# Feed-forward weights of a hybrid decoder trunk: one step of a weight strip at each of four places of a unit instead of three steps at each of two

## The chip, the cores and the metric

The kernel runs on one core of a Trainium2 chip. The metric is the device time of one execution in microseconds. Five engines work side by side, each through its own row of instructions in order: TensorE (PE, with PEld for its weight loads), VectorE (DVE), ScalarE (ACT), GpSimd (POOL) and SyncE (SP), which here mostly issues loads. An instruction that waits for another engine holds up all that stand behind it in its row.

## What is computed

One inference step of a decoder trunk of two layers, over 1048 positions in all (1024 prompt tokens, 16 meta tokens, and one token each of 8 running sequences). Each layer is a mixer (an SSD in layer 0, an RG-LRU in layer 1) and a feed-forward part, each inside norms and a residual. The change lies in the feed-forward part:

```python
D_MODEL = 1024
D_FF = 4 * D_MODEL

def sq_relu_mlp(x, w1, w2):
    h = jax.nn.relu(x @ w1)
    return (h * h) @ w2

# in trunk, behind the mixer of layer i
h = rms_norm(x, p["norm_ffn_pre"][i])
x = x + rms_norm(sq_relu_mlp(h, p["ffn_w1"][i], p["ffn_w2"][i]), p["norm_ffn_post"][i])
```

All inputs are f32. w1 is 1024 x 4096, w2 is 4096 x 1024.

## The kernel before

**Numbers as pairs.** A matrix goes to PE as two f16 matrices, a high part (the scaled value rounded to f16, written by ACT) and a low part (what the rounding left, written by DVE, which must read the high part first). A product is three matmuls: high by high, high by low, low by high. The scale of a weight strip is a power of two from the strip's largest entry.

**Tiles.** Positions stand in three pieces c of 350, 350 and 348 columns (`WC`). Weights come in strips of 256 output columns, 128 x 2048 in f32, 1 MB; a layer's feed-forward part has 32 of them. The hidden layer is worked through in four blocks b of 1024 columns: four strips of w1 make the block H, and four strips of w2 take it into `acc`. Except in the first block's w1 strips (`first_phase`, line 619, and a loop behind it) and the last block's w2 strips (`last_phase`, line 570), the work is done in units: `unit` (line 1357) is the product of one strip with one piece c by seven products of half-blocks in place of eight. Of the w1 strips (kind "H", b = 1 to 3) all four pairs of half-blocks go that way, 7 x 12 = 84 matmuls; of the w2 strips (kind "S", b = 0 to 2) two pairs do (`NSUM`), and the rest is added as ordinary products (`quadrant`), 90 matmuls. A matmul of a unit has 175 columns (174 for the last piece). The seven products go in the order 1, 6, 5, 7, 3, 4, 2 into four result buffers of PSUM, and there are eight such buffers, two units' worth. Between them ACT copies the first product into z (p1), and DVE adds the others up in z, in five or six rows: those are the rows `z<-z,mm` and `z<-mm,z`. Behind a unit of a w1 strip comes `square` (ReLU, square, the parts H, and for half the strips the sums HT that POOL makes in `t_sums`), behind one of a w2 strip an addition into `acc`.

**What a strip needs ahead of its units.** The generator `wlane` prepares strip after strip, in `wconv` (line 299), and every `yield` in it ends a step. In order: the load by SP into `ws` (two buffers, so a load waits until the strip two earlier has been split); the largest entry by DVE (`rm`, or `r4`, `r4s` and `rm` for kinds S and 2, where four parts have scales of their own); in `strip_scale` (line 267) a matmul that spreads that maximum over the partitions (`mm<-ident,rm`) and a chain of small DVE rows from `wgb` to the scales; for units, in `sums` (line 354), three quarters of the strip as high parts on ACT and low parts on DVE (`wp`), then four rows of POOL that turn the strip in `ws`, in place, into the sums that the unit's other products need; then in `split` (line 282) the whole strip as `wh`, the high part on ACT, which has to wait for POOL, and the low part in halves on DVE, which wait for ACT. For kind H that is one piece of 2048; for kinds S and 2 four pieces of 512. A finished strip goes into `ready`, and `wneed` takes it from there, running steps at once if there is none. `ahead` limits how many may stand ready.

**What sets the order.** All lanes are generators (the weight lane `wlane`, the sums of POOL, norms). `tick` (line 130) moves each of them by one step, and the weight lane by `wsteps` steps: 1 in general, 3 in the feed-forward part (set in line 1251, set back in `lru`). A unit calls `tick` once behind product 7, and `ffn` calls it once behind the unit: six steps of the weight lane a unit, 18 in the three units that a strip serves. A strip of kind H has 12 steps, of kind S 10, of kind 2 seven, of kind h (the first block's w1) three. `first_phase` and `last_phase` tick behind every group of products. The written order is not quite the order of the rows: every call goes through `Queue` (line 80 on), so all operations carry line 91, and a scheduler then settles the row of each engine.

## Time and profile before

| | |
|---|---|
| median of 3 runs | 2867.76 us (2867.46 to 2871.3) |
| the profiled execution, its own time | 2878.27 us |
| its span in the trace | 2876.5 us |
| mean granted clock of PE | 0.964 |
| unit stretch of layer 0 (first to last matmul of a unit) | 1094.75 to 1676.69, 581.94 us |
| unit stretch of layer 1 | 2183.70 to 2766.74, 583.04 us |
| PE busy over the span | 2601.7 us (90%) |
| DVE busy over the span | 2173.1 us (76%) |
| ACT, POOL busy over the span | 1322.5 us (46%), 662.3 us (23%) |
| loads of a strip, issue to landing | 64 of 1024 KB, 4.9 us |

Times in the trace run from the start of the span. A row of a view names the engine, the operation, the tile written and those read (without buffer numbers), the shape, and in brackets how long the engine stood idle just before and what ended that. Matmuls are pipelined, so the sum of their single durations is more than the time that they take together; the pace of a row of matmuls is read from the starts.

### The profile page before, as it was taken

Reading aid. Unit: us, or ns where it says so; the run is one execution under the profiler, and the core shown is the slowest. Engines: PE = TensorE matmul, PEld = TensorE weight load, DVE = VectorE, ACT = ScalarE, POOL = GpSimd, SP = SyncE. Lnnn points to the kernel's source line nnn. Section 1 sums busy time; section 2 is a strip of 40 time slices with the busy share of each in tenths; the row PEclk is TensorE's granted clock in tenths of the full one; section 3 lists DMA queues with packets and bytes.
Section 4 is the critical chain, followed back from the end, with each engine's and each line's share of the span. In section 5 each row is a group of like instructions: output and inputs, shape, how many; then the busy total and the mean of one; then the engine's idle time right before and its main releaser. Section 6 shows DMA issues by size and latency. Waiting matters only on the chain.

```text
span 2876.5 us, 56770 instructions
## 1 busy us (share of the span) xinstructions
PE 2601.7 (90%) x23318; PEld 2073.5 (72%) x23318; DVE 2173.1 (76%) x5152; ACT 1322.5 (46%) x2148; POOL 662.3 (23%) x863
## 2 busy tenths in 40 slices
PE   5999999999999999879789899989999889889888
PEld 2666666666666669879789866655668888879866
DVE  6888977897764887678688689678787678677666
ACT  4544455455544364352342444577564353352342
POOL 3212211221111025431321200132024531221101
PEclk9999999999999999999989999999999999999999
DMA  3233233322345221111121033111221101011122
GB/s 141 78 105 111 86 103 111 110 86 102 110 175 218 98 76 40 37 45 45 40 85 69 31 109 123 60 39 49 101 92 43 45 31 60 31 45 45 45 72 93
DMA packets 52756, 229.14 MB, mean 80 GB/s; under 512 B 9056, under 2 KB 18416, under 8 KB 31632
## 3 DMA queue, kind: packets, MB, share of 16 engines
q1 hardware_dynamic: 46112, 190.81, 19.2%
q0 software_dynamic: 6384, 34.71, 3.0%
q8 instruction: 182, 2.98, 0.4%
q14 instruction: 78, 0.64, 0.1%
HBM read 186.28 MB, written 39.22 MB: 78 GB/s over the span
## 4 chain that ended last, share of the span: by engine, by line
DVE 33%; PE 30%; ACT 11%; POOL 10%; DMA 8%; issue 8%; SPq 0%; POOLq 0%; DVEq 0%; ACTq 0%
PE mm L91 25%; POOL ws L91 7%; DMA ws<-w 6%; DVE z L91 5%; DVE wh L91 4%; ACT wh L91 3%; PE yo L91 2%; DVE conv L91 2%; DVE wp L91 2%; ACT z L91 2%; DVE U L91 2%; DVE L L91 2%; DVE rm L91 2%; DVE xr L91 2%; POOL z L91 1%
## 5 line engine op out<-in xcount | busy, mean ns | idle before, releaser
L91 PEld LDWEIGHTS <-wh 128*128 128x128 f16 x17040 | 1499.8, 99 | 536.0 <-issue 105.2
L91 PE MATMUL mm<-U,wh 128*128 128x350 f16 (+3 forms) x7056 | 998.0, 298 | 18.7 <-ACT rr L91 11.7
L91 PE MATMUL mm<-H,wh 128*128 128x175 f16 (+5 forms) x5664 | 560.8, 254 | 11.5 <-DVE z L91 11.5
L91 PEld LDWEIGHTS <-wp 128*128 128x128 f16 x3888 | 322.3, 101 | 47.0 <-issue 23.3
L91 POOL TENSOR_TENSOR ws<-ws 128x256 f32<-128x256 f32 (+1 forms) x192 | 210.2, 1095 | 622.1 <-DVE wp L91 593.5
L91 DVE TENSOR_TENSOR z<-z,mm 128x175 f32<-128x175 f32 (+3 forms) x648 | 227.2, 371 | 49.1 <-ACT z L91 42.6
L91 PE MATMUL mm<-U,wp 128*128 128x175 f16 (+1 forms) x1728 | 154.1, 247 | 25.3 <-DVE z L91 25.2
L91 DVE SCALAR_TENSOR_TENSOR wh<-ws,s,wh 128x256 f16<-128x256 f32 x256 | 148.8, 628 | 23.5 <-ACT wh L91 23.4
L91 PE MATMUL mm<-TT,wh 128*128 128x175 f16 (+1 forms) x1728 | 160.8, 242 | 5.3 <-DVE wh L91 4.5
L91 DVE SCALAR_TENSOR_TENSOR wh<-ws,sq,wh 128x1024 f16<-128x1024 f32 x48 | 61.5, 1281 | 111.8 <-ACT wh L91 111.8
L91 DVE SCALAR_TENSOR_TENSOR wh<-ws,sw,wh 128x1024 f16<-128x1024 f32 x94 | 117.5, 1279 | 26.4 <-ACT wh L91 26.4
L91 ACT ACTIVATE z<-z,ti 128x700 f32<-128x700 f32 (+1 forms) x72 | 62.9, 874 | 149.8 <-DVE z L91 149.8
L91 DVE TENSOR_REDUCE rm<-ws 128x1 f32<-128x2048 f32 x40 | 91.3, 2284 | 51.7 <-DMA ws<-w 46.5
L91 PE MATMUL mm<-ident,rm 128*128 128x128 bf16 x99 | 22.4, 228 | 107.6 <-DVE z L91 71.4
L91 ACT ACTIVATE pre<-mm,undo 128x8 f32<-128x8 f32 (+1 forms) x104 | 46.6, 476 | 153.9 <-PE mm L91 153.9
L91 ACT ACTIVATE wh<-ws,s 128x512 f16<-128x512 f32 x128 | 85.4, 711 | 68.2 <-POOL ws L91 60.5
L91 DVE SCALAR_TENSOR_TENSOR conv<-pre,ssmall,conv 128x1072 f32<-128x1072 f32 x78 | 105.8, 1357 | 0.0
L91 PE MATMUL mm<-H,wp 128*128 128x175 f16 (+1 forms) x864 | 90.5, 241 | 16.3 <-DVE z L91 16.3
L91 ACT ACTIVATE wh<-ws,sw 128x2048 f16<-128x2048 f32 x47 | 93.7, 1998 | 16.9 <-DVE sw L91 14.7
L91 DVE TENSOR_SCALAR L<-L,ncs 128x128 f32<-128x128 f32 (+1 forms) x288 | 94.5, 372 | 8.9 <-DMA L<-csd 8.9
L91 DVE TENSOR_TENSOR ss<-ss,sqt 128x350 f32<-128x350 f32 (+3 forms) x154 | 76.4, 502 | 32.7 <-ACT sqt L91 31.7
L91 ACT ACTIVATE wh<-ws,sq 128x2048 f16<-128x2048 f32 x24 | 48.0, 2002 | 108.3 <-POOL ws L91 108.3
(284 smaller groups left out, 4234.1 us busy)
## 6 DMA issues: line engine op xcount, KB each, us to landing
ws<-w SPq DMA_DIRECT2D x64, 1024.0 KB, 4.9
ws<-w_ssd_in SPq DMA_DIRECT2D x24, 1024.0 KB, 7.0
L<-csd SPq DMA_DIRECT2D x64, 256.0 KB, 3.3
ws<-w_lru_in SPq DMA_DIRECT2D x12, 1024.0 KB, 4.8
xd<-xc POOLq DMA_DIRECT2D x6, 1400.0 KB, 5.0
xc<-xd SPq DMA_DIRECT2D x6, 1400.0 KB, 6.2
h<-ssd_h SPq DMA_DIRECT2D x8, 1024.0 KB, 4.9
bc<-bcd SPq DMA_DIRECT2D x8, 1024.0 KB, 4.9
```

The costliest lines, as they stand in the source:

```text
L91: r = f(*args, **kw)
```

## The change

`wsteps` is gone: `tick` moves every lane by one step. A new `wtick` moves the weight lane alone by one step, and `unit` calls it behind products 6 and 4, so that a unit has four places with a step each (behind products 6, 7 and 4, and behind the unit): 12 steps in three units. `first_phase` and `last_phase` of the feed-forward part have one step of the weight lane a tick in place of three.

A strip's steps are cut differently. The spreading matmul is split off `strip_scale` into `spread_max`, with a step's end between it and the small rows for the kinds of the feed-forward part. In `split` all high parts are one step and the low parts follow in one step (kinds H and h) or two (kinds S and 2), where a high part and its two low parts alternated. In `sums` the three pairs of kind H keep a step each; the two groups of kind S are one step together; the four rows of POOL are one step, with one empty step behind them. Steps now: H 9, S 9, kind 2 six, kind h four. The operations, their shapes and their number are the same.

```diff
@@ -123,17 +123,19 @@
         self.lanes = []
         self.last_tab = None
         self.mmi = 0
-        self.wsteps = 1
         self.yfs = {}
 
 
     def tick(self):
 
         for lane in list(self.lanes):
-            for _ in range(self.wsteps if lane is self.wl else 1):
-                if next(lane, self) is self:
-                    self.lanes.remove(lane)
-                    break
+            if next(lane, self) is self:
+                self.lanes.remove(lane)
+
+    def wtick(self):
+
+        if self.wl in self.lanes and next(self.wl, self) is self:
+            self.lanes.remove(self.wl)
 
     def drain(self):
         while any(l is not self.wl for l in self.lanes):
@@ -264,14 +266,19 @@
         self.nc.sync.dma_start(st, src)
         return st
 
-    def strip_scale(self, gmax):
-
+    def spread_max(self, gmax):
+
+
+        ps = self.mm()[:, :P]
+        self.nc.tensor.matmul(ps, gmax.bitcast(BF16)[:, 1:2].to_broadcast([P, P]), self.ident.bitcast(BF16)[:, 1::2],
+                              start=True, stop=True)
+        return ps
+
+    def strip_scale(self, spread):
 
         nc, ty = self.nc, self.tiny
-        ps = self.mm()
-        nc.tensor.matmul(ps[:, :P], gmax.bitcast(BF16)[:, 1:2].to_broadcast([P, P]), self.ident.bitcast(BF16)[:, 1::2], start=True, stop=True)
         gb = ty.tile([P, 1], F32, tag="wgb", name="wgb")
-        nc.vector.tensor_reduce(gb, ps[:, :P], axis=AX.X, op=OP.max)
+        nc.vector.tensor_reduce(gb, spread, axis=AX.X, op=OP.max)
         s, p = self.pow2(gb, 1, ty, "w")
         inv = ty.tile([P, 1], F32, tag="winv", name="winv", bufs=8)
         nc.vector.tensor_scalar(inv, p, 2.0 ** -14, None, op0=OP.mult)
@@ -285,8 +292,11 @@
         for i in range(parts):
             sl = slice(i * step, (i + 1) * step)
             nc.scalar.activation(w[:, 0, sl], st[:, sl], AF.Copy, scale=s[:, i:i + 1])
-            yield
+        yield
+        for i in range(parts):
             h = step // 2
+            if i == 2:
+                yield
             for o in (i * step, i * step + h):
                 nc.vector.scalar_tensor_tensor(w[:, 1, o:o + h], st[:, o:o + h], s[:, i:i + 1], w[:, 0, o:o + h],
                                                op0=OP.mult, op1=OP.subtract)
@@ -327,7 +337,10 @@
             nc.vector.tensor_tensor(r4s, r4, rj, op=OP.mult)
             nc.vector.tensor_reduce(rm, r4s, axis=AX.X, op=OP.max)
         yield
-        s, inv, gb = self.strip_scale(rm)
+        spread = self.spread_max(rm)
+        if kind in "hH2S":
+            yield
+        s, inv, gb = self.strip_scale(spread)
         yield EARLY
         if kind != "a":
             w = new("wh")
@@ -371,13 +384,13 @@
                 nc.vector.scalar_tensor_tensor(lo, a, sk, hi, op0=OP.mult, op1=OP.subtract)
                 if parts == 1:
                     yield
+        if parts > 1:
             yield
         tt = nc.gpsimd.tensor_tensor
         for o, a, b, op in ((q(1, 1), q(1, 1), q(1, 0), OP.add), (q(1, 0), q(0, 0), q(1, 0), OP.subtract),
                             (q(0, 0), q(1, 1), q(0, 0), OP.subtract), (q(0, 1), q(0, 1), q(0, 0), OP.subtract)):
             tt(o, a, b, op=op)
-            if npair == 4:
-                yield
+        yield
         yield
 
     def product(self, ps, i, w, B, T, npair):
@@ -1248,7 +1261,6 @@
         HT = fp.tile([P, 3, NSUM, 3, 2, CW // 2], F16, name="HT")
         U = self.U
         sctx = ExitStack()
-        self.wsteps = 3
         for b in range(4):
             H = fp.tile([P, 3, KT, 2, CW], F16, tag="H", name="H")
             rs = {}
@@ -1381,12 +1393,14 @@
             if i == 6:
                 nc.scalar.activation(p1, pa[:, 0], AF.Copy)
                 nc.vector.tensor_tensor(u2, p1, pa[:, 1], op=OP.add)
+                self.wtick()
             if i == 7:
                 nc.vector.tensor_tensor(xy, pb, zv[:, 2:3].to_broadcast([P, 2, n]), op=OP.add)
                 nc.vector.tensor_tensor(u2, c12, pb[:, 1], op=OP.add)
                 self.tick()
             if i == 4:
                 nc.vector.tensor_tensor(xy, xy, pc, op=OP.add)
+                self.wtick()
         if npair < 4:
             self.chain(pd[:, 1], self.quadrant(w[0], B, npair, 1, 1))
         nc.vector.tensor_tensor(p1, p1, pd[:, 0], op=OP.add)
@@ -1396,7 +1410,6 @@
 
 
     def lru(self):
-        self.wsteps = 1
         nc, tc, ty = self.nc, self.tc, self.tiny
         a, v = self.a, self.v
         sctx = ExitStack()
```

Three places in DVE's row show what the scheduler made of it. Numbers in the names are those of buffers; they differ between the two programs for the same thing.

The first place is the third w1 strip of b = 1 in layer 0. `wp` and `wh` are the low parts of this strip, z_13553 the last unit of the strip in use, z_13673 and z_13797 (z_13799) the units behind it, mm the results of PE. DVE before, from two rows ahead of the last `wp` on:

```order
L91 TENSOR_TENSOR H_13295<-z_13553,H_13295 128x174
L91 TENSOR_TENSOR z_13673<-z_13673,mm_13670 128x175
L91 SCALAR_TENSOR_TENSOR wp_13729<-ws_13353,sq4_13730,wp_13729 128x512
L91 TENSOR_TENSOR HT_10777<-z_13553,HT_10777 128x3x174
L91 TENSOR_TENSOR z_13673<-z_13673,mm_13671 128x2x175
L91 TENSOR_TENSOR z_13673<-z_13673,mm_13672 128x175
L91 SCALAR_TENSOR_TENSOR wh_13728<-ws_13353,sq4_13730,wh_13728 128x1024
L91 TENSOR_TENSOR z_13797<-z_13797,mm_13793 128x175
L91 SCALAR_TENSOR_TENSOR wh_13728<-ws_13353,sq4_13730,wh_13728 128x1024
```

And DVE in the change, from the last `wp` on:

```order
L91 SCALAR_TENSOR_TENSOR wp_13703<-ws_13327,sq4_13704,wp_13703 128x512
L91 TENSOR_TENSOR z_13673<-z_13673,mm_13669 128x175
L91 TENSOR_TENSOR H_13295<-z_13553,H_13295 128x174
L91 TENSOR_TENSOR H_13295<-z_13553,H_13295 128x348
L91 TENSOR_TENSOR z_13673<-mm_13670,z_13673 128x2x175
L91 TENSOR_TENSOR z_13673<-z_13673,mm_13670 128x175
L91 TENSOR_TENSOR z_13673<-z_13673,mm_13671 128x2x175
L91 TENSOR_TENSOR H_13295<-z_13553,H_13295 128x174
L91 SCALAR_TENSOR_TENSOR wh_13702<-ws_13327,sq4_13704,wh_13702 128x1024
L91 TENSOR_TENSOR HT_10777<-z_13553,HT_10777 128x3x174
L91 TENSOR_TENSOR z_13673<-z_13673,mm_13672 128x175
L91 SCALAR_TENSOR_TENSOR wh_13702<-ws_13327,sq4_13704,wh_13702 128x1024
```

The last `wp` row, behind which POOL's four rows may run, has moved up past three rows of z_13673 and three H rows of z_13553, which now stand between it and the first `wh` row, and `HT` has moved from ahead of the first `wh` row to behind it. On POOL the four rows on `ws` stand ahead of the sums of z_13553 now, and behind them before.

The second place is the beginning of the unit stretch of layer 0: ws_11513 is the second w2 strip of b = 0, z_11715 (z_11696 in the change) the first unit of the first w2 strip, z_11851 the unit behind it, r the hidden values of the first block. DVE before:

```order
L91 SCALAR_TENSOR_TENSOR wp_11747<-ws_11513,s4_11752,wp_11747 128x128
L91 TENSOR_TENSOR H_10778<-r_11600,H_10778 128x2x350
L91 SCALAR_TENSOR_TENSOR wp_11747<-ws_11513,s4_11752,wp_11747 128x128 x5
L91 SCALAR_TENSOR_TENSOR wh_11746<-ws_11513,s4_11752,wh_11746 128x256 x8
L91 TENSOR_TENSOR z_11715<-z_11715,mm_11711 128x175
L91 TENSOR_TENSOR z_11715<-mm_11712,z_11715 128x2x175
L91 TENSOR_TENSOR H_10778<-r_11680,H_10778 128x2x348
L91 TENSOR_TENSOR z_11715<-z_11715,mm_11712 128x175
```

In the change:

```order
L91 SCALAR_TENSOR_TENSOR wp_11824<-ws_11513,s4_11829,wp_11824 128x128 x2
L91 TENSOR_TENSOR z_11696<-z_11696,mm_11695 128x175 x2
L91 SCALAR_TENSOR_TENSOR wp_11824<-ws_11513,s4_11829,wp_11824 128x128 x4
L91 TENSOR_TENSOR z_11851<-z_11851,mm_11847 128x175
L91 TENSOR_TENSOR z_11851<-mm_11848,z_11851 128x2x175
L91 SCALAR_TENSOR_TENSOR wh_11823<-ws_11513,s4_11829,wh_11823 128x256
L91 TENSOR_TENSOR z_11851<-z_11851,mm_11848 128x175
L91 SCALAR_TENSOR_TENSOR wh_11823<-ws_11513,s4_11829,wh_11823 128x256
L91 TENSOR_TENSOR U_9864<-f_11884,U_9864 128x175
L91 SCALAR_TENSOR_TENSOR wh_11823<-ws_11513,s4_11829,wh_11823 128x256 x3
L91 TENSOR_TENSOR z_11851<-z_11851,mm_11849 128x2x175
L91 SCALAR_TENSOR_TENSOR wh_11823<-ws_11513,s4_11829,wh_11823 128x256 x2
```

Before, all `wp` and `wh` rows of the second strip stand ahead of the first z row of the first unit; in the change they stand between the z rows of the first two units (the eighth `wh` row comes two rows later).

The third place lies in the w2 strips of b = 1 in layer 0: the last `r4` row reads a strip (ws_15146, in the change ws_15132) that is loaded into the buffer from which the strip two earlier (wh_14782, in the change wh_14768) has been split. z_14751 and z_14887 (z_14884) are units of the w2 strip in use. DVE before:

```order
L91 TENSOR_TENSOR z_14751<-z_14751,mm_14748 128x175
L91 SCALAR_TENSOR_TENSOR wh_14782<-ws_14450,s4_14788,wh_14782 128x256
L91 TENSOR_TENSOR z_14751<-z_14751,mm_14749 128x2x175
L91 SCALAR_TENSOR_TENSOR wh_14782<-ws_14450,s4_14788,wh_14782 128x256 x2
L91 TENSOR_TENSOR r4s_14995<-r4_14922,rj_13148 128x4
L91 TENSOR_REDUCE rm_14921<-r4s_14995 128x1
L91 TENSOR_TENSOR z_14751<-z_14751,mm_14750 128x175 x2
L91 SCALAR_TENSOR_TENSOR acc_10776<-z_14751,iq4_14456,acc_10776 128x700
L91 TENSOR_TENSOR z_14887<-z_14887,mm_14883 128x175
L91 TENSOR_TENSOR z_14887<-mm_14884,z_14887 128x2x175
L91 TENSOR_TENSOR z_14887<-z_14887,mm_14884 128x175
L91 TENSOR_REDUCE r4_15288<-ws_15146 128x2
```

In the change:

```order
L91 SCALAR_TENSOR_TENSOR wh_14768<-ws_14424,s4_14774,wh_14768 128x256 x5
L91 TENSOR_TENSOR z_14751<-z_14751,mm_14750 128x175 x2
L91 SCALAR_TENSOR_TENSOR wh_14768<-ws_14424,s4_14774,wh_14768 128x256
L91 SCALAR_TENSOR_TENSOR acc_10776<-z_14751,iq4_14430,acc_10776 128x700
L91 TENSOR_TENSOR z_14884<-z_14884,mm_14880 128x175
L91 SCALAR_TENSOR_TENSOR wh_14768<-ws_14424,s4_14774,wh_14768 128x256
L91 TENSOR_TENSOR z_14884<-mm_14881,z_14884 128x2x175
L91 TENSOR_TENSOR z_14884<-z_14884,mm_14881 128x175
L91 TENSOR_TENSOR z_14884<-z_14884,mm_14882 128x2x175
L91 TENSOR_REDUCE r4_15325<-ws_15132 128x2
```

The last `wh` row, which sets the load free, has moved from ahead of the last rows of z_14751 to behind the first row of the next unit, and the `r4` row that waits for the load has stayed within a row of where it was. SP's row holds the same loads in the same order in both.

## The prediction

> **What bounds the kernel now.** I began with the views that set the whole apart from its stages: the page's first line, then the busy time of each engine in the two stretches in which the units of the feed-forward part run (the two rows under it: stretch, its length, then busy time and instructions of PE, PEld, DVE, ACT and POOL, the granted clock, the DMA share, GB/s).
>
> ```profile
> span 2876.5 us, 56770 instructions
> 1094.75:1676.69 581.94, 506.37 (x6290) 499.69 (x6288) 436.50 (x1056) 223.11 (x393) 176.04 (x210) 0.94 0.15 52
> 2183.70:2766.74 583.04, 508.09 (x6290) 500.15 (x6288) 429.32 (x1051) 222.54 (x392) 175.90 (x210) 0.95 0.13 45
> ```
>
> The two stretches are 1165 of 2876.5 us, and only they, and the few us at their edges, are touched by the change in a way that can count: the rows of the SSD and LRU stages stand as before. The reader is to see that no engine is busy all the time, neither PE (506 of 582, and a busy PE includes slow matmuls) nor DVE (436). So the next view is the waits in the first stretch: engine, operation, what released it, us, times, longest.
>
> ```profile
> PE mm L91 <- DVE z L91: 59.3, 27, 8.1
> PE mm L91 <- DVE rm L91: 14.9, 4, 7.0
> DVE wh L91 <- ACT wh L91: 63.5, 22, 6.3
> DVE z L91 <- ACT z L91: 20.6, 18, 2.0
> DVE rm L91 <- DMA ws<-w: 16.6, 8, 3.0
> DVE r L91 <- DMA ws<-w: 5.8, 5, 2.0
> DVE z L91 <- PE mm L91: 2.1, 2, 1.3
> ```
>
> PE waits for DVE; DVE hardly ever waits for PE (2.1 us in 2 places). So **the row of DVE's work, its busy time plus its waits for ACT, POOL and DMA, is the stage**: 436.5 busy and some 145 idle, of which the 63.5 for ACT's high parts is the largest piece. Whatever shortens or lengthens that row counts, and PE follows. What the 63.5 is made of, the groups of DVE's instructions show (count, busy, mean ns, idle before).
>
> ```profile
> L91 DVE SCALAR_TENSOR_TENSOR wh<-ws,sq,wh 128x1024 f16<-128x1024 f32 x24 | 30.7, 1281 | 55.5 <-ACT wh L91 55.5
> L91 DVE SCALAR_TENSOR_TENSOR wh<-ws,s,wh 128x256 f16<-128x256 f32 x95 | 58.2, 654 | 8.1 <-ACT wh L91 8.1
> L91 DVE SCALAR_TENSOR_TENSOR wp<-ws,s,wp 128x128 f16<-128x128 f32 x60 | 18.6, 348 | 1.6 <-ACT wp L91 1.6
> L91 DVE TENSOR_TENSOR z<-z,mm 128x175 f32<-128x175 f32 x167 | 52.4, 331 | 14.1 <-ACT z L91 12.9
> L91 DVE TENSOR_TENSOR HT<-z,HT 128x522 f16<-128x522 f32 x4 | 5.8, 1445 | 0.9 <-ACT HT L91 0.8
> L91 DVE TENSOR_TENSOR HT<-z,HT 128x525 f16<-128x525 f32 x8 | 5.6, 705 | 5.0 <-ACT HT L91 5.0
> ```
>
> Twelve H strips (24 halves) cost 55.5 us of waiting, 4.6 each. One of them in order of time, the third of b=1 (start, us, engine, operation, count, idle before):
>
> ```profile
> 1226.40 0.81 DVE L91 SCALAR_TENSOR_TENSOR wp<-ws,sq,wp 128x512 f16<-128x512 f32 x1
> 1226.53 1.08 PE L91 MATMUL mm<-U,wh 128*128 128x174 f16 x12 [0.68 <-DVE z L91]
> 1227.34 5.63 POOL L91 TENSOR_TENSOR ws<-ws 128x512 f32<-128x512 f32 x4 [0.68 <-ACT HT L91]
> 1227.37 1.81 DVE L91 TENSOR_TENSOR HT<-z,HT 128x522 f16<-128x522 f32 x1 [0.16 <-ACT HT L91]
> 1227.45 1.07 PE L91 MATMUL mm<-TT,wh 128*128 128x174 f16 x12
> 1233.01 2.00 ACT L91 ACTIVATE wh<-ws,sq 128x2048 f16<-128x2048 f32 x1 [2.25 <-POOL ws L91]
> 1235.04 1.28 DVE L91 SCALAR_TENSOR_TENSOR wh<-ws,sq,wh 128x1024 f16<-128x1024 f32 x1 [5.20 <-ACT wh L91]
> 1236.63 0.26 PE L91 MATMUL mm<-ident,rm 128*128 128x128 bf16 x1 [8.11 <-DVE z L91]
> 1236.69 1.94 PE L91 MATMUL mm<-U,wh 128*128 128x174 f16 x12
> ```
>
> After DVE's last low part of the sums come 5.63 us of POOL and 2.00 of ACT: DVE needs 7.6 us of other work before its first wh row. What stands there I call the cover; here 2.3 us, and the wait is the rest. PE goes on until its result buffers are full and then stands for 8.11.
>
> **The change part by part.** No instruction is added or removed (the same maxima, copies, sums and matmuls), no new wait is written; all of it is order. So each term is DVE work moved into or out of a cover.
>
> *The chain of the H strips.* I laid the cover of all twelve strips side by side in the two orders, at the group means. A layer has 35.1 us before and 34.9 after: the third strip of b=1 gains 0.6 (seven z and H rows, 2.90, for HT and two z, 2.29), the last of b=3 gains 2.4, the fourth of b=1 loses 2.9 and that of b=2 1.7 (2.9 in the second layer). The largest wait of the stage is thus left where it is: +0.2 in layer 0 and +1.4 in layer 1, **+1.6**.
>
> *The reload of ws.* A strip may be loaded when the low parts of the strip two earlier are done, and its maximum is the next thing DVE wants:
>
> ```profile
> 1304.22 0.87 DVE L91 SCALAR_TENSOR_TENSOR wh<-ws,s,wh 128x256 f16<-128x256 f32 x2
> 1305.24 0.33 SPq L264 DMA_DIRECT2D ws<-w  x1
> 1305.27 0.58 DVE L91 TENSOR_TENSOR z<-z,mm 128x175 f32<-128x175 f32 x2
> 1305.88 0.95 DVE L91 SCALAR_TENSOR_TENSOR acc<-z,iq,acc 128x700 f32<-128x700 f32 x1
> 1306.75 0.33 DVE L91 TENSOR_TENSOR z<-z,mm 128x175 f32<-128x175 f32 x1
> ...
> 1310.12 1.22 DVE L91 TENSOR_REDUCE r<-ws 128x2 f32<-128x1024 f32 x1 [2.03 <-DMA ws<-w]
> ```
>
> From issue to the maximum are 4.9 us. Eight rows, 3.10 us at the group means, lie between, and the wait is 2.03. In the new order three z rows (1.36 us) lie there: 1.7 more of waiting. The same sum for the two strips ahead of it goes from 6.41 to 3.92 and from 4.29 to 2.91; against 4.9 us that adds 0.9 and 1.4. Together 4.0 at this place, and the same order stands at b=1 and b=2 of layer 1: **+12** for three places. The order of the loads on SP's queue doesn't change. Bounds: nothing, if the waits move into one another, and +17 if the lost cover counts in full (2.5+1.4+1.7, three times).
>
> *The second S strip of b=0.* Before, it is converted while the units have not yet begun to wait for DVE:
>
> ```profile
> 1087.85 0.29 DVE L91 TENSOR_REDUCE wgb<-mm 128x1 f32<-128x128 f32 x1 [4.10 <-PE mm L91]
> 1091.11 1.40 DVE L91 SCALAR_TENSOR_TENSOR wp<-ws,s,wp 128x128 f16<-128x128 f32 x5
> 1094.75 0.62 PE L91 MATMUL mm<-H,wp 128*128 128x175 f16 x6
> 1096.88 3.01 DVE L91 SCALAR_TENSOR_TENSOR wh<-ws,s,wh 128x256 f16<-128x256 f32 x4 [1.38 <-ACT wh L91]
> 1099.82 0.33 DVE L91 TENSOR_TENSOR z<-z,mm 128x175 f32<-128x175 f32 x1
> ```
>
> DVE had waited 4.10 for PE just before, so that work was partly free. At one step a tick it slides into units 0 and 1, where DVE is the bound. It is 6 x 0.35 + 8 x 0.65 = 7.3 us. DVE's first z row then comes as soon as the first two products and ACT's copy of one are there, some 1.7 us after PE's start at 1094.75 (an estimate: twice the 0.62, and half a microsecond for the copy), which is 3.4 earlier than 1099.82. ACT's part moves as well and stands ahead of the copies for which z waits, two more waits at the mean of the row above (20.6 / 18 = 1.1). 7.3 - 3.4 + 2.3 = 6.2 a layer, **+12.4**. Bounds: 0 (PE fills its buffers meanwhile and DVE catches up) and +19 (nothing of the 3.4 is kept). The other strips of the first phase, and those of the last, now at one step a tick too, I cost at nothing: PE is what DVE waits for there (the 4.10); without that cover a late strip would cost its 7.3.
>
> *Waits that go.* At the second H strip of b=1 the wh rows now fall between two units, and this wait behind them lapses, with the H row's behind it: 2.2 a layer, **-4.4**.
>
> ```profile
> 1206.31 0.34 DVE L91 TENSOR_TENSOR z<-z,mm 128x175 f32<-128x175 f32 x1 [1.97 <-ACT z L91]
> ```
>
> HT of the third H strip of b=1 and b=2 runs under POOL's chain now (1.81 above; the four of that width mean 1.445 against 0.705 for the eight others) and stands behind the first wh row in the new order: 4 x 0.74, **-3.0**. [...] Late next is then POOL's sums for that HT, now queued behind the ws chain; they are needed by the S units only.
>
> At the end of a unit stage PE meets the matmul that spreads the maximum of the last strip before that maximum is there:
>
> ```profile
> 1684.23 0.29 PE L91 MATMUL mm<-ident,rm 128*128 128x128 bf16 x1 [5.98 <-DVE rm L91]
> 1684.32 5.78 PE L91 MATMUL mm<-H,wh 128*128 128x350 f16 x26
> ```
>
> In the new order it stands 20 matmuls of 350 columns later. Twelve of half the width take 0.92 (1226.53 to 1227.45), so these are 20 x 0.153 = 3.1 us: about 3 each, **-6**. The other two rm stalls of the 14.9 stand at b=2 of layer 0, where DVE itself idled little for the strip; the order is more favourable there, **-2**.
>
> The sum: 1.6 + 12 + 12.4 - 4.4 - 3.0 - 6 - 2 = +10.6. The profiled execution took 2878.27 (its span 2876.5 and 1.8 around it); 2888.9 by its own measure. It lies 10.5 above the median of 2867.76 of the runs, which the forecast is for: **2878**. With the low ends of the two unknown terms the sum is -14 (2854), with the high ends +22 (2890); I widen by some 4 for the covers taken at means: 2850 to 2895.
>
> **The rivals.** *The units run as the change lays them out, and DVE's long waits go under PE's time.* With one step at four places DVE does little between two z rows, PE's buffers come free evenly, and POOL's 7.6 us pass while PE still has buffers. For it: DVE's row has 436 us in it and PE's matmuls 6264 x 0.077 = 482, so 100 us of the stretch belong to neither. Against it: the cover before the wh rows is the same, and DVE never waits for PE, so even spacing alone frees nothing. If the longest stall of PE (8.11) goes at b=1 and b=2 in both layers, with the slow matmuls behind each (1.94 for 1.08, some 2.9 until the pace is back), that is 4 x 11 = 44 us: 2824; half of it 2846. [...]
>
> *PE's lead is lost.* The spread matmul now stands behind two products of the third unit of a strip, not four: 24 matmuls, 1.83 us, earlier on PE's queue, with every later product queued behind it. PE waits there if the maximum is late; at 1.83 x 24 strips a layer that is 44 us a layer at most. It decides where the maximum comes later than PE's lead over DVE, as in the four stalls of 14.9 us. If a quarter of the 48 strips meet it in full, +22 on top of the sum: 2900.
>
> *The order comes out the same in what counts*: gains and losses of DVE's row cancel, since the chain of 7.6 us stays: 2868.
>
> **How the numbers follow.** The forecast 0.50, the evenly fed PE 0.28, the lost lead 0.14, no effect 0.08. A measurement of this kernel tells about 0.2% (5.7 us) from no change. Within its own spread the forecast is slower in 0.31, within that bound in 0.14, faster in 0.05. So faster 0.05 + 0.28 = 0.33, the same 0.14 + 0.08 = 0.22, slower 0.31 + 0.14 = 0.45. The range reaches into both rivals, 2838 to 2902; outside are half of the faster one (0.14) and a third of the slower one.
>
> **What would show it.** In the groups of DVE: wh 128x1024 with about 55 us of idle before it in either layer (right) or under 35 (the first rival). The r and rm rows with some 4 us more of DMA wait in the w2 strips of b=1. Unit 0 with wp and wh rows of a strip between its z rows, and the stretch from its first matmul longer by some 6 us. HT 128x522 at 0.7 in four of eight places. The waits of PE for rm: fewer at the ends of the stretches, or, by the second rival, many short ones. The forecast is wrong if DVE begins to wait for PE for tens of us: then DVE is no longer the bound.

## The result, and the profile after

| | before | with the change |
|---|---|---|
| median | 2869.53 us (2867.46 to 2873.61, 4 runs) | 2904.8 us (2897.21 to 2910.72, 4 runs) |
| ratio | 1 | 1.012, 95% interval 1.0091 to 1.0148 |
| the profiled execution, its own time | 2878.27 us | 2897.21 us |
| unit stretch of layer 0 | 581.94 us | 592.78 us |
| unit stretch of layer 1 | 583.04 us | 594.94 us |

The change makes the kernel 1.2% slower, by 35 us, where 10 were forecast. The two profiled executions lie 18.7 us apart in span, but they differ ahead of the feed-forward part already: the last matmuls of the SSD stage came 7.9 us earlier in the execution of the change, though nothing there was changed (over all runs of this case the first unit begins between 1087 and 1097 us). So what follows, from the first unit on, accounts for 18.7 + 7.9 = 26.6 us of the 35; the other 9 are in no trace (the profiled execution of the change was the shortest of its four, that of the kernel before longer than its four) and stay open.

The windows of the change over its two unit stretches; columns as before (length, busy time and count of PE, PEld, DVE, ACT, POOL, granted clock, DMA share, GB/s):

```profile
1086.86:1679.64 592.78, 509.21 (x6292) 504.04 (x6290) 443.23 (x1074) 224.91 (x398) 171.93 (x206) 0.94 0.15 51
2188.60:2783.54 594.94, 511.58 (x6291) 506.85 (x6290) 433.81 (x1071) 224.57 (x398) 172.74 (x206) 0.93 0.12 44
```

Each stretch is 11 to 12 us longer and holds 4.5 to 6.7 us more of DVE work and 4 to 7 more of DVE idle time. Part of that work came in from the first phase: over the whole span DVE is busy for 2170.4 us, where it was 2173.1. Which waits changed, the groups of DVE over the whole span show (busy, mean ns, idle before and what ended it). Before:

```profile
L91 DVE TENSOR_TENSOR z<-z,mm 128x175 f32<-128x175 f32 (+3 forms) x648 | 227.2, 371 | 49.1 <-ACT z L91 42.6 <-PE mm L91 1.3
L91 DVE SCALAR_TENSOR_TENSOR wh<-ws,s,wh 128x256 f16<-128x256 f32 x256 | 148.8, 628 | 23.5 <-ACT wh L91 23.4
L91 DVE TENSOR_REDUCE r<-ws 128x2 f32<-128x1024 f32 x64 | 77.1, 1212 | 18.5 <-DMA ws<-w 18.3
L91 DVE TENSOR_TENSOR H<-z,H 128x175 f16<-128x175 f32 (+5 forms) x120 | 72.4, 620 | 31.9 <-ACT z L91 20.3 <-ACT H L91 11.3
L91 DVE SCALAR_TENSOR_TENSOR wh<-ws,sq,wh 128x1024 f16<-128x1024 f32 x48 | 61.5, 1281 | 111.8 <-ACT wh L91 111.8
L91 DVE TENSOR_TENSOR HT<-z,HT 128x525 f16<-128x525 f32 (+1 forms) x24 | 22.9, 953 | 13.0 <-ACT HT L91 12.9
```

With the change:

```profile
L91 DVE TENSOR_TENSOR z<-z,mm 128x175 f32<-128x175 f32 (+3 forms) x648 | 228.8, 371 | 62.1 <-ACT z L91 56.4
L91 DVE SCALAR_TENSOR_TENSOR wh<-ws,s,wh 128x256 f16<-128x256 f32 x256 | 142.3, 597 | 32.0 <-ACT wh L91 31.6
L91 DVE TENSOR_TENSOR H<-z,H 128x175 f16<-128x175 f32 (+5 forms) x120 | 82.5, 704 | 36.9 <-ACT z L91 18.1 <-ACT H L91 18.0
L91 DVE TENSOR_REDUCE r<-ws 128x2 f32<-128x1024 f32 x64 | 77.2, 1214 | 35.2 <-DMA ws<-w 35.2
L91 DVE SCALAR_TENSOR_TENSOR wh<-ws,sq,wh 128x1024 f16<-128x1024 f32 x48 | 61.1, 1281 | 89.0 <-ACT wh L91 89.0
L91 DVE TENSOR_TENSOR HT<-z,HT 128x525 f16<-128x525 f32 (+1 forms) x24 | 18.0, 752 | 12.2 <-ACT HT L91 12.2
```

From the first list to the second: the wait for the H strips' high parts fell by 22.8 us, HT is 4.9 cheaper, and the low parts of the w2 strips (`wh` 128x256) are 6.5 cheaper. Against that the H rows cost 10.1 more of busy time, the maxima r wait 16.7 longer for the reload, the low parts of the w2 strips 8.5 longer, nearly all of it for ACT, and the z rows wait 13 longer. Of these 13, 11 are one wait of 5.59 at the first unit of each layer, which is shown below. PE's waits in the unit stretch of layer 0 are all for DVE's z and rm now (what it waited for, us, times, longest); together they are 83.5, where the kernel before has 75.5:

```profile
PE mm L91 <- DVE z L91: 74.2, 24, 8.7
PE mm L91 <- DVE rm L91: 9.3, 2, 5.3
```

Where the first units of layer 0 begin, DVE stands idle three times, 18 us in all (start, us, operation, idle before). It waits for ACT there, and ACT for PE: ahead of its copies r, ACT stood idle 3.0 us for PE's products.

```profile
1075.04 0.89 DVE L91 TENSOR_TENSOR H<-r,H 128x700 f16<-128x700 f32 x1 [6.28 <-ACT r L91]
1082.19 0.89 DVE L91 TENSOR_TENSOR H<-r,H 128x700 f16<-128x700 f32 x1 [6.26 <-ACT r L91]
1088.67 0.34 DVE L91 TENSOR_TENSOR z<-z,mm 128x175 f32<-128x175 f32 x1 [5.59 <-ACT z L91]
```

In the same stretch the kernel before has the 4.10 that the prediction showed and one more:

```profile
1082.87 0.89 DVE L91 TENSOR_TENSOR H<-r,H 128x700 f16<-128x700 f32 x1 [6.28 <-ACT r L91]
```

And the reload at the place that the prediction worked out, in the w2 strips of b=1:

```profile
1309.61 0.47 DVE L91 SCALAR_TENSOR_TENSOR wh<-ws,s,wh 128x256 f16<-128x256 f32 x1
1310.01 0.51 DVE L91 TENSOR_TENSOR z<-mm,z 128x350 f32<-128x350 f32 x1
1310.55 0.96 DVE L91 TENSOR_TENSOR z<-z,mm 128x175 f32<-128x175 f32 x2
1314.99 1.22 DVE L91 TENSOR_REDUCE r<-ws 128x2 f32<-128x1024 f32 x1 [3.48 <-DMA ws<-w]
```

Three z rows stand between the last low part and the maximum, as the order showed, and the wait is 3.48 in place of 2.03.

Where in the stretch the time goes, DVE's row shows at the first z row of the last unit of b=0 (the last of three pieces of the fourth w2 strip). Before, and with the change:

```profile
1187.70 0.34 DVE L91 TENSOR_TENSOR z<-z,mm 128x174 f32<-128x174 f32 x1 [1.15 <-ACT z L91]
```

```profile
1189.06 0.34 DVE L91 TENSOR_TENSOR z<-z,mm 128x174 f32<-128x174 f32 x1 [0.39 <-ACT z L91]
```

That is 92.95 us behind the first matmul of a unit before, and 102.20 with the change: 9.2 of the 10.8 us by which the stretch of layer 0 grew are lost in b=0. In layer 1 it is 9.6 of 11.9.

### The profile page after: what moved, and what is told of

Its sections match the earlier page's. It is cut to its first block, busy times and chain, and to the rows that moved or that the text cites. A ratio compares the mean times of both kernels' runs of the same rounds, so it can differ in the third digit from the quotient of the medians.

```text
span 2895.2 us, 56781 instructions
## 1 busy us (share of the span) xinstructions
PE 2600.8 (90%) x23318; PEld 2081.5 (72%) x23318; DVE 2170.4 (75%) x5152; ACT 1324.1 (46%) x2148; POOL 662.1 (23%) x863
## 5 line engine op out<-in xcount | busy, mean ns | idle before, releaser
L91 PEld LDWEIGHTS <-wh 128*128 128x128 f16 x17040 | 1521.5, 100 | 600.4 <-issue 188.9
L91 PE MATMUL mm<-H,wh 128*128 128x175 f16 (+5 forms) x5664 | 570.9, 257 | 8.9 <-DVE z L91 8.8
L91 PEld LDWEIGHTS <-wp 128*128 128x128 f16 x3888 | 309.9, 99 | 7.5 <-DVE z L91 4.9
L91 PE MATMUL mm<-ident,rm 128*128 128x128 bf16 x99 | 22.9, 233 | 175.2 <-DVE z L91 143.7
L91 DVE SCALAR_TENSOR_TENSOR wh<-ws,s,wh 128x256 f16<-128x256 f32 x256 | 142.3, 597 | 32.0 <-ACT wh L91 31.6
L91 PE MATMUL mm<-U,wp 128*128 128x175 f16 (+1 forms) x1728 | 146.7, 241 | 2.4 <-DVE z L91 2.4
L91 DVE TENSOR_TENSOR H<-z,H 128x175 f16<-128x175 f32 (+5 forms) x120 | 82.5, 704 | 36.9 <-ACT z L91 18.1
L91 DVE TENSOR_REDUCE r<-ws 128x2 f32<-128x1024 f32 x64 | 77.2, 1214 | 35.2 <-DMA ws<-w 35.2
```

The lines of the kernel that those rows point to most:

```text
L91: r = f(*args, **kw)
```

## The experiments

In the kernel as it is printed, `split` begins in line 280, `wconv` in 294, `sums` in 359 and `unit` in 1367. All times are medians of 4 to 12 runs beside runs of the kernel before on the same chip, whose medians were 2871.3 to 2871.8. Theory A: work was moved from a time in which DVE waits for PE into the units. Theory C: PE's lead over DVE is lost, since the spreading matmul stands earlier (the second rival of the prediction). Later theories are named where they come up.

### The first phase's pace put back

```diff
             if b == 0:
+                self.wsteps = 3
                 self.first_phase([self.wneed() for _ in range(3)], act, evac)
...
+                self.wsteps = 1
                 tl = self.input_sums(U, TT, fp)
```

(`tick` moves the weight lane by `wsteps` again; the units keep their four places.)

> The change with the weight lane back at three steps a tick in the first block's first phase and in the loop behind it, so that the second w2 strip of b=0 is converted ahead of the units as before; the units keep four places of one step. Theory A (the work of that strip was moved from a time in which DVE waits for PE into the units): DVE's row to the first w1 strip of b=1 loses 9 us in each layer, 18 in all: about 2887 against 2905, DVE idle ahead of the H rows of the first phase back from 16 us to 9 a layer. Theory C (PE's lead is lost since the spreading matmul stands behind two products and not four): no change, 2905 within 5.

Measured: 2889.36 us, ratio 1.0059 (1.0047 to 1.0072). That is 15.4 less than the change, and theory A's number within 3. Its sign came too: DVE's idle time ahead of the first phase's H rows is 9.6 and 11.9 us in the two layers, where the change has 16.5 and 17.4. The same step taken alone from the kernel before, with one step a tick in the first block and nothing else:

> The kernel before, with the first block's first phase at one step a tick and nothing else of the change. Theory A by itself: the second w2 strip of b=0 slides into the first units, 7 to 9 us a layer: 2871 + 15 = 2886, 2882 to 2890. Against it, the two runs with the old cut at four places differed by 5 us only: then 2874 to 2878, and the loss belongs to the new cut as much as to the pace.

Measured: 2882.12 us, 1.0035 (1.0022 to 1.0048): 10 us lost by the pace of the first phase alone, where 15 was expected. It is a loss by itself, and its size depends on the cut and the places (5 to 15 us in the four pairs run here).

### The spreading matmul later in PE's row

```diff
             if i == 6:
...
-                self.wtick()
             if i == 7:
+                self.wtick()
```

> The change with the step behind product 6 moved to behind product 7 (two steps there in a row): nothing between the two on DVE and ACT but one addition and one copy, and on PE the spreading matmul stands 12 or 24 matmuls later. Theory A: within 6 us of the change's 2905, PE's waits at the spreading matmul shorter by 1 to 2 us a strip and returned at the next product. Theory C: each strip gets its 1 to 1.8 us of lead back, 48 strips: 2860 to 2885.

Measured: 2905.29 us, 1.0116 (1.01 to 1.0131), the time of the change. PE's wait at those matmuls did get shorter, by 15 us over the span:

```profile
L91 PE MATMUL mm<-ident,rm 128*128 128x128 bf16 x99 | 22.7, 231 | 160.0 <-DVE z L91 127.3 <-DVE rm L91 31.8 <-ACT wh L91 0.8
```

It was 175.2 in the change and 107.6 in the kernel before. Nothing of it reached the end, where theory C asked for 20 to 45 us. By itself this is not a clean test: only 15 of the 68 us came back, and the scheduler moved DVE rows too, since the small rows behind that matmul wait for it (the H strips' wait for their high parts went from 89.0 to 112.6, the H rows from 82.5 to 72.5 busy). What speaks against theory C beside it is that the time does not follow this wait: it is 37.3 us in a run of 2878 (`f3_pool3s` below), 48.3 in one of 2859 (`f3_pool3`), 88.7 in one of 2876 (`places3`), and 107.6 in the kernel before. And in the unit stretches of the change PE is not in the list of what DVE waits for; ACT's copies z, through which PE could hold DVE up, wait for PE for 17.3 and 12.9 us there, where it was 37.2 and 26.3. So PE's stalls are where DVE's delay shows, rather than its cause.

### The cut alone and the places alone

The new cut of the steps with the old pace (three steps at two places):

```diff
             for _ in range(self.wsteps if lane is self.wl else 1):
...
+        self.wsteps = 3
         for b in range(4):
...
             if i == 6:
...
-                self.wtick()
...
             if i == 4:
...
-                self.wtick()
```

> The new cut of a strip's steps alone, with the old pace: three steps a tick at two places. Theory A: the first phase is served as before, so the 18 us of b=0 are gone; what is left against the kernel before is the longer wait for the reload and for the high parts of w2 strips: 2875 to 2890. Theory C: the spreading matmul is again late in PE's row, so all the loss is gone: 2870 within 4.

Measured: 2897.96 us, 1.0092 (1.0078 to 1.0105), 8 us above A's range and 24 above C's. One new wait stands out in it: DVE's U rows wait 34.2 us for ACT's U, where the kernel before has 1.5. ACT's U copies in turn wait 49.7 us for POOL's f, where the kernel before has 16.9:

```profile
L91 DVE TENSOR_TENSOR U<-f,U 128x175 f16<-128x175 f32 (+1 forms) x24 | 12.3, 513 | 34.2 <-ACT U L91 34.2
L91 ACT ACTIVATE U<-f 128x175 f16<-128x175 f32 (+1 forms) x24 | 8.3, 344 | 49.7 <-POOL f L91 49.7
```

POOL's row says why. Its rows f, from which ACT makes U, stand behind the four rows on a strip in it or between them, and those had waited for DVE's low parts (start, us, operation, idle before):

```profile
1111.11 3.15 POOL L91 TENSOR_TENSOR ws<-ws 128x256 f32<-128x256 f32 x4 [6.83 <-DVE wp L91]
1114.22 1.53 POOL L91 TENSOR_TENSOR f<-U 128x350 f32<-128x350 f16 x2
```

With the four places this is gone again: U waits 5.4 us in the change.

The old cut with the new places, on the kernel before:

```diff
-        self.wsteps = 3
         for b in range(4):
...
             if i == 6:
...
+                self.wtick()
...
             if i == 4:
...
+                self.wtick()
```

> The old cut of the steps with one step at each of four places. Theory A: the first phase has one step a tick, so the 18 us of b=0 stay, and with 12 places for a strip of 12 steps the H strips finish late: 2890 to 2915. Theory C: the spreading matmul and its chain are one step again and stand where the pace puts them; where that is behind 60 to 90 matmuls of the third unit PE keeps its lead and the time is 2870 to 2880.

Measured: 2880.96 us, 1.0034 (1.0021 to 1.0047). It is 9 us below A's range and 1 above C's, so it speaks against A's size; beside the change it says that the new cut costs 24 us at the new places.

### Which part of the cut

Starting from the old cut at four places, with the first phase's pace put back (`places3`):

> The old cut of the steps, one step at each of four places of a unit, and three steps a tick in the first block's first phase. If theory A's loss (second w2 strip of b=0 pushed into the units, 15 us in the pair of the change and the run with the first phase restored) adds to any cut: 2881 - 15 = 2866, 2861 to 2871, no slower than the kernel before. If it came about only with the new cut: 2880.

Measured: 2876.41 us, 1.0015 (1.0001 to 1.0029), 10 above the expected 2866 and nearer to the other case. On that, once the new `sums` and once the new `split`, each word for word as in the change:

```diff
                 if parts == 1:
                     yield
+        if parts > 1:
             yield
...
             tt(o, a, b, op=op)
-            if npair == 4:
-                yield
+        yield
         yield
...
             nc.scalar.activation(w[:, 0, sl], st[:, sl], AF.Copy, scale=s[:, i:i + 1])
-            yield
+        yield
+        for i in range(parts):
             h = step // 2
+            if i == 2:
+                yield
```

> As the run with the old cut, four places and the first phase restored, but with the new sums: POOL's four rows in one step with one empty step behind them, two steps between them and the split of an H strip, not five. Theory D (the new cut loses because the H strips' split comes too early, so DVE waits longer for POOL and ACT): DVE's wait of wh for ACT's wh up by 15 us over both layers, the time up by 12 to 18. Theory E (it loses because ACT's four high parts of a w2 strip come in one piece and hold up ACT's other copies): within 4 of the run it starts from.

> As the run with the old cut, four places and the first phase restored, but with the new split: all high parts in one step, the low parts in one or two behind it. Theory E: 8 to 15 us more, in waits for ACT (z, H, U) and in r for the reload. Theory D: within 4 of the run it starts from.

Measured: 2886.11 us, 1.0046 (1.0033 to 1.006) with the new `sums`, and 2866.69 us, 0.9978 (0.9966 to 0.9989) with the new `split`. Theory E falls: the new `split` gains 10 us. The new `sums` loses 10, somewhat less than theory D said, and D's reason fails: DVE's wait for the H strips' high parts went down, from 86.0 to 77.3, and not up by 15. What went up is the H rows, from 81.8 to 88.7 busy and from 32.0 to 44.7 idle.

The third part of the cut, the step between the spreading matmul and the small rows, was not run alone. With all three parts the time is 2889.36 (the first run above), 13 us over the 2876.41 of the old cut, while `sums` and `split` alone cancel; so 13 us belong to that step or to the meeting of the parts, and which is open.

### Empty steps put back behind POOL's rows

`sums` before the change had five steps' ends between POOL's first row and the split of an H strip; the change has two. On the change with the first phase's pace put back (`f3_pool3`):

```diff
             tt(o, a, b, op=op)
         yield
         yield
+        if npair == 4:
+            yield
+            yield
+            yield
```

> The change with the first phase restored, and three more empty steps between POOL's rows and the split of an H strip, five in all as in the old cut. Theory D: DVE's wait of wh for ACT's wh falls from 123 us to about 105 over both layers, time 2889 to about 2872. Theory E: within 5 of 2889.

Measured: 2859.46 us, 0.9955 (0.994 to 0.9969). Three empty steps take 30 us off, more than D's 17, and make a kernel 12 us faster than the one before. Its groups of DVE, and behind them two of the run without the empty steps:

```profile
L91 DVE TENSOR_TENSOR z<-z,mm 128x175 f32<-128x175 f32 (+3 forms) x648 | 228.8, 370 | 43.7 <-ACT z L91 36.0 <-PE mm L91 0.7
L91 DVE SCALAR_TENSOR_TENSOR wh<-ws,s,wh 128x256 f16<-128x256 f32 x256 | 153.1, 644 | 18.6 <-ACT wh L91 18.5
L91 DVE TENSOR_REDUCE r<-ws 128x2 f32<-128x1024 f32 x64 | 77.1, 1211 | 26.9 <-DMA ws<-w 26.9
L91 DVE TENSOR_TENSOR H<-z,H 128x175 f16<-128x175 f32 (+5 forms) x120 | 76.7, 656 | 34.3 <-ACT H L91 19.4 <-ACT z L91 14.9
L91 DVE SCALAR_TENSOR_TENSOR wh<-ws,sq,wh 128x1024 f16<-128x1024 f32 x48 | 61.1, 1281 | 100.6 <-ACT wh L91 100.6
```

```profile
L91 DVE SCALAR_TENSOR_TENSOR wh<-ws,s,wh 128x256 f16<-128x256 f32 x256 | 145.0, 612 | 32.3 <-ACT wh L91 32.0
L91 DVE TENSOR_REDUCE r<-ws 128x2 f32<-128x1024 f32 x64 | 77.2, 1213 | 42.4 <-DMA ws<-w 42.4
```

That run has 49.8 of waiting ahead of the z rows, 89.0 ahead of the H strips' low parts and 82.5 of busy H rows. So with the empty steps the H strips' own wait is 11.6 longer, and the waits of r, of the w2 low parts and of z are shorter by 15.5, 13.7 and 6.1, the H rows by 5.8; against that the w2 low parts are busy 8.1 longer and HT waits 5.7 longer. The steps don't shorten the wait for POOL. That they keep the lane from getting ahead, so that the next strips' reload, split and ACT copies fit, agrees with these waits, but is not shown by itself.

The same three steps on the whole change, the first phase at one step a tick:

> The change as it is, first phase at one step a tick, with three more empty steps between POOL's rows and the split of an H strip. If the two losses add (15 us by the first phase, 30 by the missing steps): 2905 - 30 = 2875, 2870 to 2880.

Measured: 2874.55 us, 1.0014 (1.0004 to 1.0024). The two losses add, as expected.

### How many steps, and where

All of these stand on the change with the first phase's pace put back. Three empty steps ahead of an H strip's maximum, none behind POOL's rows:

```diff
             if self.specs[i][1] in "hH2S":
+                if self.specs[i][1] == "H":
+                    yield
+                    yield
+                    yield
                 conv = self.wconv(*staged.pop(i))
```

> The change with the first phase restored and three empty steps for each H strip ahead of its maximum, not behind POOL's rows: 12 steps a strip as in the run with five steps between POOL's rows and the split, but the split is as close to POOL's rows as in the change. Theory F (a strip with 9 steps for its 12 places runs ahead and bunches, so any three steps cure it): 2858 to 2866. Theory D (the distance between POOL's rows and the split is what counts): 2885 to 2895.

Measured with three empty steps ahead of the maximum: 2875.81 us, 1.0015 (1.0005 to 1.0026), 14 of the 30 us. Neither theory D nor F holds alone.

The others are the same two edits in other numbers: one step behind POOL's rows; two there and one ahead of the maximum; four there, with the `yield` behind `spread_max` taken out; three there for S strips too (without the `if npair == 4`).

> The change with the first phase restored and one more empty step between POOL's rows and the split of an H strip. Theory D: the H rows of the split move behind one more place, a third of the 30 us of three steps or more: 2870 to 2882. Theory F: a third of the spare places filled: the same 2870 to 2882; a step function would be 2889 or 2860.

Measured with one empty step behind POOL's rows: 2887.58 us, 1.0057 (1.0045 to 1.0069), 2 us less than without, where both theories asked for a third of the 30. One step does next to nothing.

> 12 steps for an H strip, but four of them between POOL's rows and the split and one ahead of its maximum. Runs so far: 2859 with three steps behind POOL's rows, 2876 with none there and three ahead. If both count in proportion: a third of the way, 2865, 2862 to 2868. If the last step decides (with one step behind POOL's rows the time hardly moved): above 2870.

Measured with two empty steps behind POOL's rows and one ahead of the maximum: 2869.29 us, 0.9991 (0.9981 to 1.0001), 60% of the way from 2859 to 2876, where a third was expected if both count in proportion and 2870 or more if the last step decides. It lies between the two cases: the last of the three steps behind POOL's rows counts more than its third.

> The fast run with the step between the spreading matmul and the small rows taken out and put behind POOL's rows: 12 steps for an H strip again, six of them between POOL's rows and the split. Theory D (distance): 2 to 6 us less, 2853 to 2858. Theory F (12 steps are all that counts): 2859 within 3. If the small rows then wait for PE's matmul: wgb behind PE up by 5 us or more and 2862 or above.

Measured with four behind POOL's rows and the step behind the spreading matmul taken out: 2864.35 us, 0.9969 (0.9958 to 0.998). 5 us more than with that step, at the edge of what these runs tell apart, and above the ranges of both theories; `wgb` waits 22.8 us for PE where it was 22.6, so the small rows did not pay. r is back at 32.2 us of waiting and the w2 low parts at 29.1. The edit takes that step from the S strips too (nine steps to eight), so it does not weigh the H strips alone.

> The change with the first phase restored and three more empty steps behind POOL's rows for H and S strips both, 12 steps each. Theory D: the S strips wait for POOL too (wh 128x256 behind ACT, 18 us of the 123), so 2846 to 2856. Theory F: S strips stay behind in the lane and their waits for the reload fall as well: 2840 to 2856. Either is wrong if an S strip is late for its unit: PE waits for wh, above 2865.

Measured with S strips stretched to 12 steps as well (`f3_pool3s`): 2878.37 us, 1.0027 (1.0016 to 1.0039), 19 us slower than with the H strips alone. Both theories are wrong there, and by the sign that was named for it: the S strips come late for their units. PE's waits for wh go from 61.0 us (36.6 for ACT's, 24.4 for DVE's) to 86.1 (52.3 and 33.8). Of DVE's waits, that of rm for its load went from 49.3 to 57.9 us.

### The last phase's pace

```diff
             else:
+                self.wsteps = 3
                 sctx.close()
```

(on the run with three empty steps behind POOL's rows)

> The fast run (the change with the first phase restored and five steps between POOL's rows and the split of an H strip) with three steps a tick in the last phase too. If the w2 strips of the last block come late at one step a tick, PE's wait for their maximum goes: 2 us a layer, 2855. If the last phase hides the pace: 2859 within 3.

Measured: 2860.48 us, 0.9961 (0.9947 to 0.9975), the same as with one step a tick. The last phase hides the pace.

A third buffer for the strips, which would bear on the wait for the reload alone, was not run.

## Why the prediction was wrong

**What bounds the kernel** was right. In the changed kernel DVE's waits that lead back to PE lie at the edge of the first phase; inside the unit stretches PE is not in the list of what DVE waits for.

**The sum by place.** The two traces hold 26.6 us of the loss. In b=0 DVE falls back by 9.2 and 9.6 us, 18.8 in all, where 12.4 was forecast. From there to PE's last matmul of a unit the two layers add 1.6 and 2.3; the terms for that part (+1.6, +12, -4.4, -3.0, -2) come to +4.2, so their sum came out. That is luck, since several of them did not, as the paragraphs below show. Behind the units it is +3.7 where -6 was forecast. So in the traces the sum missed at its two edges, by 6 and by 10 us, and some 9 more lie between the traces and the medians.

**The reload** was right: +12 was forecast, with 0.9, 1.4 and 1.7 us at the three strips of a place. In layer 0, b=1, the waits are 1.2, 2.1 and 3.5 us where they were 0.1, 0.9 and 2.0, which is 3.7 against the forecast 4.0. Layer 1 has 3.8 at b=1 and 5.4 at b=2, and b=2 of layer 0 has 1.5: 14.4 in all.

**The second S strip of b=0** was right in mechanism and a little too small. From its first z row to the first z row of the last unit of that block, DVE fell back by 12.5 us in layer 0 and 12.8 in layer 1, from which the earlier start of 3.3 (forecast: 3.4) goes: 9.2 and 9.6, where 6.2 was worked out. In the block DVE has the strip's 14 wp and wh rows more (6.8 us by their single durations), small rows of two scales more, and U and TT rows that are 1.3 longer. As DVE's rows overlap a little (where one begins before the one ahead of it has ended, it does so by 0.08 us, the median in either trace), these make 7.9 us together; 4.6 and 5.0 are waits, where 2.3 were counted. With the first phase's pace put back DVE is still 2.7 and 1.7 us behind at the same row. So 14.4 of the 18.8 go with the pace, and the rest with the new cut. The runs put the pace at 10 us (alone), 15 (in the change) and 5 (at the four places with the old cut).

**The end of the unit stage** was wrong in sign: -6 forecast, because the spreading matmul stands 20 matmuls later. From the last matmul of a unit to the last one of the block's H products it takes 99.3 and 99.5 us, where it was 97.5 and 97.6. PE stands for DVE's maximum there in any case, 4.95 us in layer 0 and 7.43 in layer 1, where it was 5.98 and 5.99:

```profile
1696.25 0.29 PE L91 MATMUL mm<-ident,rm 128*128 128x128 bf16 x1 [4.95 <-DVE rm L91]
```

The DVE row, not PE's, sets when that maximum comes: the term gave PE's row a price that the prediction itself said belongs to DVE's.

**HT and the H rows**: HT moved out from under POOL's chain, and gained 4.9 where 3.0 was forecast. But the H rows that moved under the chain lost 10.1. For one shape: 128x696 rows of H took 0.88 on average before and 1.13 after; with the change four of the 16 stand beside POOL's rows on ws and took 1.91, the other twelve 0.88. The term was -3.0 and measures +5.2. The z rows, which read a result of PE, kept their mean of 371 ns. The term holds what HT gains by the move and nothing for what the H rows lose by it.

**The chain of the H strips** is the step whose reasoning failed. It was laid down as left where it is, +1.6, by the cover between two rows of a strip. Its wait fell by 22.8 us, and what the change did to the H strips came out elsewhere. The prediction compared the rows of one strip; it did not ask what a strip of 9 steps does in 12 places, where 12 steps had filled 12. In the runs three empty steps put back into the H strips are worth 30 us, more than all the terms of the sum together, with the first phase's pace put back and without it. A little under half of it comes from the number of steps alone, the rest from where they stand. A likely reading is that such a strip ends early and the lane goes on to the next, whose maximum, split and copies on ACT come at times when their data aren't there; but which row of which engine carries the loss was not settled. All that is shown is that the waits of r, of the w2 low parts and of z shrink while that of the H strips grows. Nor is a missing step worth the same everywhere: with the old `split`, H strips of 8 steps cost 10 us against 12 steps.

**The waits said to go** were not measured apart. DVE's row through the H units of b=1, which holds them together with the strips' chains and the H and HT rows, is 3.4 and 3.3 us shorter in the two layers, and that of b=2 2.8 in layer 0, where the two rm stalls stood, and 1.0 in layer 1.

**What the sum left out** is the low parts of the w2 strips behind ACT, +8.5: the step with four high parts at once was costed as a mere change of order.

**The rivals.** The faster one asked that PE's buffers come free evenly and DVE's long waits go under PE's time. Its price was a little high: the 2.9 for the slow matmuls behind a stall was an estimate that no run shows. Behind the stall of 8.11 the next 48 matmuls took 5.57 us (1236.69 to 1242.26), where four times the 0.92 of twelve is 3.68: they lost 1.9, which makes 40 us in place of its 44. The kernel of 2859 gains 12 us with the four places, but not by its sign: the H strips' wait is 100.6 us there, 50 a layer, where it asked for under 35. The slower one named the right sign and, by the runs above, the wrong mechanism. The sum's ends (2850 to 2895) and the range up to 2902 didn't hold 2904.8.

So by the runs the change's 33 us (2904.8 against the 2871 to 2872 of the kernel before in these runs) are about +15 for the first phase's pace, +30 for the H strips' missing steps, and -12 for the four places with the rest of the cut. The first was in the sum at 12.4; for the other two together, +18, the sum had -1.8. This is one order of adding up: taken from the old cut at four places, the same parts have other sizes.

## What to carry to other kernels

Where software lanes are moved by ticks, the number of steps of a unit of work against the number of ticks in which it is used is a quantity of its own, and no comparison of neighbouring rows shows what it is worth. It has to be run, and for each kind of work: here three more steps made the H strips 30 us faster, and three more for the S strips too took 19 of them back. When a pace is lowered, look for the stretch in which the waiting engine had idle time to give, and keep the old pace there. When rows are moved under a long chain of another engine as cover, count what they lose by running beside it (here 10.1 us of the H rows) as well as what they hide.

## What the runs showed of the hardware

Beside POOL's rows on ws some of DVE's rows took up to three times their length and others took no longer. With the change, five of the eight H rows of 128x348 stand beside them and took 1.60 us, the other three 0.51 (1.19 on average of the eight); the rows `z<-z,mm` of 128x350, which read a result of PE, took 0.51 in either case. Nor did each H row pay: before the change two of 128x696 beside POOL's rows on ws took their usual 0.88. What sets these rows apart was not shown. A wait that names ACT came from further back here: with the cut alone, DVE's U rows wait 34.2 us for ACT's copies, and these wait 49.7 us for rows of POOL that stand behind others in its row.
